# Two transformer parts on one core: attention tasks spaced by one step, a later request for a norm factor, another order in the channel sums

## The chip, the core and the metric

The kernel runs on one core of a Trainium2 chip. TensorE (PE) multiplies matrices, VectorE (DVE) and ScalarE (ACT) work element by element, GpSimd (POOL) does a few small powers, and SyncE (SP) starts the weight transfers. Each engine takes its instructions in program order and waits on semaphores where an operand or a buffer isn't ready. The metric is the time of one execution on the device, in microseconds; the kernel before has been timed in three runs.

## What is computed

The input is 256 tokens of width 1024 in float32. Two blocks follow each other. The first has two layers, each an attention and a gated feed-forward net with a convolution over three tokens; the second layer's attention has 16 query heads, 4 key heads, a window of 128 tokens and a learned "sink" in the softmax. The second block mixes a gated delta rule with a retention and ends with a plain feed-forward net; the change touches it only in one sum.

```python
def rmsnorm(x, g):
    xf = x.astype(jnp.float32)
    y = xf * lax.rsqrt(jnp.mean(xf * xf, axis=-1, keepdims=True) + EPS)
    return (y * g.astype(jnp.float32)).astype(x.dtype)
...
    m = jnp.maximum(jnp.max(logits, axis=-1, keepdims=True), sink)
    e = jnp.exp(logits - m)
    p = e / (jnp.sum(e, axis=-1, keepdims=True) + jnp.exp(sink - m))
    out = jnp.einsum('bkgnqp,bknpd->bkgnqd', p.astype(v.dtype), vcat)
...
    u = conv_b + sum(conv_w[j] * up[:, j:j + S_] for j in range(CONV_W))
    gate, val = jnp.split(u, 2, axis=-1)
    return (jax.nn.silu(gate) * val) @ w_down
...
        x = x + o.transpose(0, 2, 1, 3).reshape(B_, S_, N_HEADS * HEAD_DIM) @ w_o
        x = x + conv_ffn(rmsnorm(x, ffn_norm[l]), w_up[l], conv_w[l], conv_b[l], w_down[l])
```

## The kernel before

**Weights.** Every weight comes by DMA in halves of 512 KB (`raw`). ACT rounds a half to `hi` (L192), DVE takes the rest as `lo` (L201, two instructions of 512 columns a half), and PE multiplies three times: hi by high part, hi by low part, lo by high part of the other operand (`OH`/`OL` or `XH`/`XL`). A chunk of weights is four *pieces*; a piece is 12 matmuls of 128 x 256 (L138). The pieces form one long list, in the order in which PE takes them.

**Tasks beside the list.** All else (norms, attention, gates) is written as Python generators. After every piece each active generator is advanced by one step; `pause(n)` lets n pieces go by. So the numbers in the tables at the top of the file are delays in pieces, and the order on each queue comes from them.

**Attention.** `attend` handles a pair of heads. A task first waits `delay + 1` steps (`N_AD0` for the first attention, `N_AD1` for the second). Then, in one step: *qk*, the scores on PE, two banks; the masked maximum on DVE (L625, an instruction and a read of its result, four times, then `nm`, L629); the exponentials on ACT (L633), and for the second attention the sinks' (`es`, L637). Two steps later comes the scaling *S* on DVE (sum with `es` L641, reciprocal L643, four multiplications L146). A step later *T*: six transposes on PE (L149), which ACT copies to `pT` (L142). A step later *PV* on PE, a copy `o` and its rounding `OH` on ACT (L142, L467), and another step later `OL` on DVE (L469). `e` and `pT` lie in one ring of tiles, "h", of `HB` = 6. The second attention's eight tasks belong to four chunks of queries of two tasks each; a chunk's tasks begin when its product is finished and DVE has rotated it (*rope*, L582 to L585, into `qk`).

**Norms.** The squares of the channels are summed over partitions by matmuls with a column of ones: `sum_ch`, for each half of the tokens (`t`) and each quarter of it (`j`, 32 tokens), adds up the three parts that `Norm` keeps. `stat` computes the factor from the sum: DVE (`tok`, L536), POOL (`RTOK`, a power, L537); then it pauses `N_STAT[n]` steps, PE transposes RTOK to a row (L149), and ACT copies it to `RB` (L541). The four factors of the first block are n0, nf0 (ahead of the first net), n1 and nf1, with `N_STAT[1]` to `[4]`; the second block begins with a double one, `stat2`, and has nmix later.

**Deferred posts and banks.** While a factor is under way, finished products can't be scaled: `wpost` puts their follow-up into `deferred`, and the next post after the factor is there, `late`, does them all. `wbank` gives the next chunk a bank of the set `ps_w` as long as fewer than two posts are deferred, and of the set `ps_d` otherwise. In the first net the follow-up of a chunk (`act`) is the multiplication by `RB` (L763), the convolution (ACT L789, DVE L793), the gate (ACT L796, DVE L798) and the split.

Of the kernel before, what the change touches and what calls it, by code (L numbers as in the profile page):

```python
# [18 lines left out]
def pause(n):  # L19
    for _ in range(n):  # L20
        yield
# [4 lines left out]
EPS = 1e-6  # L26
LEVELS = 5
LA = 3
HB = 6
RAW = 4  # L30

N_RN = (0, 1, 1, 5)
N_SY = (0, 6, 4, 4, 3)
N_STAT = (0, 3, 5, 2, 5)
N_AD0 = (4, 0, 0, 0, 0, 0, 0, 2)
N_AD1 = (3, 2, 1, 3, 0, 0, 2, 0)
N_CONV4 = (0, 1, 2, 2)
N_M1 = (1, 1, 2, 3)
MAGIC = 12582912.0
# [27 lines left out]
def body(ctx: ExitStack, tc: tile.TileContext, a):  # L67
# [10 lines left out]
    def TW(shape, tag, bufs=2, dt=F32):  # L78
        return wk.tile(shape, dt, name=tag, tag=tag, bufs=bufs)

    side = {"n": 0, "dbusy": False}
# [3 lines left out]
    def PT(tag="side"):  # L85
        if tag == "side":

            age = {t: taken[t][-BANKS[t]] if len(taken[t]) >= BANKS[t] else 0 for t in "sd"}
            tag = "s" if side["dbusy"] or deferred or age["s"] <= age["d"] else "d"
        side["n"] += 1  # L90
        taken[tag].append(side["n"])
        return ps.tile([128, 512], F32, name="ps_" + tag, tag=tag, bufs=BANKS[tag])
# [12 lines left out]
    def P_(n, i=None):  # L105
        lo, hi = PRM_O[n]
        return prm[:, lo:hi] if i is None else prm[:, lo + i:lo + i + 1]

    def C_(n):
        lo, hi = CST_O[n]  # L110
        return cst[:, lo:hi]
# [25 lines left out]
    def mm(out, lhsT, rhs, start, stop):  # L137
        PE.matmul(out, lhsT, rhs, start=start, stop=stop, skip_group_check=True)  # L138

    def cp(eng, out, in_, scale=None):  # L140
        if eng == "S":
            S.activation(out, in_, AF.Copy, scale=scale) if scale is not None else S.copy(out, in_)  # L142
        elif scale is None:
            V.tensor_copy(out, in_)
        else:
            V.tensor_scalar(out, in_, scale, None, op0=OP.mult)  # L146

    def tr(out, in_):
        PE.transpose(out, in_, ident)  # L149
# [4 lines left out]
    parts = {}  # L154
    state = {"dma": 0, "hi": 0, "lo": 0, "part": 0}
    where, last_of = {}, []
    deferred = []
# [102 lines left out]
    def drain(gen):  # L260
        while gen in active:
            step(gen)
# [12 lines left out]
    def free(*tags):  # L275
        for t in tags:
            used[t] -= 1

    def wbank(more=0):

        if len(deferred) + more >= 6:
            drain(cur["stat"])
            late()
        return PT("w" if len(deferred) + more < 2 else "d")

    def waiting():
        return cur["stat"] in active or cur.get("kv") in active

    def late(n=99):
        while deferred and n:  # L290
            deferred.pop(0)()
            n -= 1
# [21 lines left out]
    def W_chunk(src, xs, post, pre=None, bank=None):  # L314
        def m(ck, s, hi, lo):
            xh, xl = xs
            if s == 0:
                ck.bank = PT(bank) if bank else wbank()
            todo = []
            for kk in range(2):  # L320
                k = 2 * s + kk
                for f in range(2):
                    c = slice(kk * 256 + f * 128, kk * 256 + f * 128 + 128)
                    todo.append((ck.bank[:, f * T:(f + 1) * T], hi[:, c], lo[:, c], xh[:, k], xl[:, k], k == 0 and f == 0, k == 7))
            products(todo, s == 0 and 0)
        return add(Chunk(src, 2048, 4, m, pre, {3: lambda ck: wpost(post)(ck.bank)}))

    def X_chunk(src, xs, post, pre=None):
        def m(ck, s, hi, lo):
            xh, xl = xs  # L330
            if s == 0:
                ck.bank = wbank()
            todo = []
            for kk in range(2):
                k = 2 * s + kk
                for t in range(2):
                    c = slice(kk * T, kk * T + T)
                    tt = slice(t * 128, t * 128 + 128)
                    todo.append((ck.bank[:, t * T:(t + 1) * T], xh[:, k, tt], xl[:, k, tt], hi[:, c], lo[:, c], k == 0 and t == 0, k == 7))
            products(todo, True)  # L340
        return add(Chunk(src, 2048, 4, m, pre, {3: lambda ck: wpost(post)(ck.bank)}))
# [115 lines left out]
    def slots(t):  # L457
        return OH[:, t % 16], OL[:, t % 16]
# [6 lines left out]
    def split(src, hi, lo):  # L465

        S.activation(hi, src, AF.Copy)  # L467
        yield
        V.tensor_tensor(lo, src, hi.bitcast(F32), op=OP.subtract)  # L469


    class Norm:
# [16 lines left out]
        def sums(self, out):  # L489
            sum_ch(out, [self.acc[:, :T], self.sq[:, :T], self.sq[:, T:]])  # L490

    def sum_ch(out, parts):

        for t in range(2):
            for j in range(0, 128, 32):
                for i, x in enumerate(parts):
                    c = t * 128 + j
                    mm(out[j:j + 32, t:t + 1], x[:, c:c + 32], ones, i == 0, i == len(parts) - 1)

# [29 lines left out]
    def stat(norm):  # L529
# [7 lines left out]
        G.tensor_tensor(RTOK, m, mhalf[:, :2], op=OP.pow)  # L537
        yield from pause(N_STAT[n])
        p = PT("s")
# [70 lines left out]
    def attend(q, k, v, slot, window=False, sink=None, delay=0, done=False):  # L610

        yield from pause(delay + 1)
        mx = TW([128, 4], "mx", 4)
        nm = TW([128, 4], "nm", 4)
        sums = TW([128, 4], "sums", 4)
        e = [TW([128, 384], "h", HB) for _ in range(2)]
        qbs = ((0, slice(0, 128), MW[:, 128:256]), (1, slice(128, 384), MW if window else MF))
        for h in range(2):
            r = slice(64 * h, 64 * h + 64)
            b = PT()  # L620
            mm(b[:, 0:128], q[r, 0:128], k[r, 0:128], True, False)
            mm(b[:, 128:384], q[r, 128:256], k[r, 0:256], True, False)
            for qb, c, m in qbs:
                i = 2 * h + qb
                V.tensor_tensor_reduce(e[h][:, c], b[:, c], m, 0.125, -3e38 if sink is None else P_("sinks", sink + h),  # L625
                                       op0=OP.add, op1=OP.max, accum_out=mx[:, i:i + 1])
        if done:
            free("qk")
        V.tensor_scalar(nm, mx, -1.0, None, op0=OP.mult)  # L629
        for h in range(2):  # L630
            for qb, c, _ in qbs:
                i = 2 * h + qb
                S.activation(e[h][:, c], e[h][:, c], AF.Exp, bias=nm[:, i:i + 1], accum_out=sums[:, i:i + 1])  # L633
        if sink is not None:
            es = TW([128, 4], "es", 4)
            for h in range(2):
                S.activation(es[:, 2 * h:2 * h + 2], nm[:, 2 * h:2 * h + 2], AF.Exp,  # L637
                             bias=P_("sinks", sink + h))
        yield from pause(2)
        if sink is not None:  # L640
            V.tensor_tensor(sums, sums, es, op=OP.add)  # L641
        ri = TW([128, 4], "ri", 4)
        V.reciprocal(ri, sums)  # L643
        for h in range(2):
            for qb, c in ((0, slice(0, 128)), (1, slice(128, 384))):
                i = 2 * h + qb
                cp("V", e[h][:, c], e[h][:, c], ri[:, i:i + 1])
        yield from pause(1)
        pT = [TW([128, 384], "h", HB) for _ in range(2)]
        for h in range(2):  # L650
            b = PT()
            for i in range(3):
                tr(b[:, i * 128:i * 128 + 128], e[h][:, i * 128:i * 128 + 128])

            cp("S", pT[h], b[:, :384])
        yield from pause(1)
        b = PT()
        for h in range(2):
            o = slice(64 * h, 64 * h + 64)
            mm(b[o, 0:256], v(0, h), pT[h][:, 0:256], True, False)  # L660
            mm(b[o, 128:256], v(1, h), pT[h][:, 256:384], False, True)
        o = TW([128, T], "e")
        cp("S", o, b[:, :T])
        yield from split(o, *slots(slot))
# [187 lines left out]
    def q1_task(c, bank):  # L852
# [4 lines left out]
        for i in range(2):  # L857
# [3 lines left out]
                                  (lambda kt: lambda t, h: VB[:, t, (2 * kt + h) * 64:(2 * kt + h) * 64 + 64])(kt),  # L861
                                  p, True, 2 * p, N_AD1[p], i == 1))

# [415 lines left out]
    def ret_task(h):  # L1279
# [7 lines left out]
        free("qn", "qn")  # L1287
        sT = TW([128, 384], "h", HB)
        dw = C_("decw")[:, h * T:h * T + T]
# [492 lines left out]
def build(nc, arrays):  # L1782
    a = {k: nc.dram_tensor("in_" + k, v.shape, mybir.dt.from_np(v.dtype), kind="ExternalInput").ap()
         for k, v in arrays.items()}
    a["out"] = nc.dram_tensor("out_x", (2, 128, D), F32, kind="ExternalOutput").ap()
    with tile.TileContext(nc) as tc:
        body(tc, a)
# [12 lines left out]
```

## Time and profile before

| | |
|---|---|
| three runs, us | 1318.57 (median), 1314.76, 1320.49 |
| profiled execution, us | 1320.17 |
| its span, us | 1317.7 |
| PE / weight loads / DVE / ACT busy | 98% / 94% / 74% / 55% |
| mean granted clock of PE | 0.995 |
| chain that ended last | PE 91%, DVE 5%, ACT 2%, issue 1% |

The span is the stretch from the first to the last instruction; the execution's own time is 2.5 us longer. The chain that ended last follows the work back from the end, at each step to what released it. By the timeline the first net's sum nf0 is at 132 us and the second attention's first scores at 340; the second net's long sum is at 597, and the second block follows.

### The profile page before, as it was taken

The numbers are of one execution on the slowest core, as the hardware profiler recorded it, in microseconds if no ns is written. First come the engines' busy times: TensorE is split into PE (matmuls) and PEld (weight loads), VectorE is DVE, ScalarE is ACT, GpSimd is POOL, SyncE is SP. The second block draws the span as 40 slices with busy tenths as digits, with TensorE's granted clock in tenths as the row PEclk, the third lists the DMA queues.
The fourth block names the chain that finished last, engine by engine and source line by source line (L and its number), as shares of the span: only waits on it lengthen the run. The fifth ranks groups of instructions, "written<-read, shape, count | busy, mean of one in ns | idle before, by whom it ended". The sixth has DMA issues, their size and how long they took to land.

```text
span 1317.7 us, 28944 instructions
## 1 busy us (share of the span) xinstructions
PE 1290.7 (98%) x11824; PEld 1233.9 (94%) x11824; DVE 973.8 (74%) x2149; ACT 725.5 (55%) x1158; POOL 28.0 (2%) x32
## 2 busy tenths in 40 slices
PE   7999999998999999999999999999999999999998
PEld 6989999998889999998989999999999999899996
DVE  6998887778888977787778889575648556855554
ACT  5666665555665755566554454354334445655553
POOL 0000000000000000000000000000000000000000
PEclk9999999999999999999999999999999999999999
DMA  7435565554324655544333333346454554465552
GB/s 243 144 130 169 189 209 185 188 192 161 107 102 154 214 185 184 192 153 155 129 129 114 113 130 129 129 160 207 139 183 166 183 195 156 159 215 191 193 184 88
DMA packets 60468, 215.77 MB, mean 164 GB/s; under 512 B 6832, under 2 KB 7600, under 8 KB 60336
## 3 DMA queue, kind: packets, MB, share of 16 engines
q1 hardware_dynamic: 59328, 212.31, 48.4%
q8 instruction: 92, 1.51, 0.5%
q10 hardware_dynamic: 1008, 1.63, 0.4%
q14 instruction: 40, 0.33, 0.1%
HBM read 212.86 MB, written 1.05 MB: 162 GB/s over the span
## 4 chain that ended last, share of the span: by engine, by line
PE 91%; DVE 5%; ACT 2%; issue 1%; DMA 0%; POOL 0%; SPq 0%; POOLq 0%; DVEq 0%; ACTq 0%
PE ps_w L138 53%; PE ps_d L138 32%; PE ps_s L138 4%; PE ps_s L149 1%; DVE lo L201 1%; PE ps_d L149 1%; ACT h L633 1%; DMA xT<-in_x 0%; ACT hi L192 0%; DVE y L793 0%; DVE OL L690 0%; DVE XL L463 0%; DVE h L625 0%; DVE y L1399 0%; DVE REG L146 0%
## 5 line engine op out<-in xcount | busy, mean ns | idle before, releaser
L201 DVE TENSOR_TENSOR lo<-raw,hi 128x512 fp32r<-128x512 f32 x801 | 520.4, 685 | 99.2 <-ACT hi L192 98.5
L192 ACT ACTIVATE hi<-raw 128x1024 fp32r<-128x1024 f32 (+1 forms) x403 | 418.8, 1048 | 167.6 <-PE ps_w L138 81.1
L138 PE MATMUL ps_w<-XH,hi 128*128 128x256 f32 x976 | 164.4, 290 | 4.4 <-ACT hi L192 1.9
L138 PE MATMUL ps_w<-XL,hi 128*128 128x256 f32 x976 | 154.5, 280 | 0.5 <-DVE XL L1475 0.5
L138 PE MATMUL ps_w<-XH,lo 128*128 128x256 f32 x976 | 154.0, 279 | 0.0
L138 PE MATMUL ps_w<-OH,hi 128*128 128x256 f32 x896 | 144.4, 283 | 0.0
L138 PE MATMUL ps_w<-OH,lo 128*128 128x256 f32 x896 | 141.9, 280 | 0.4 <-DVE lo L201 0.4
L138 PE MATMUL ps_w<-OL,hi 128*128 128x256 f32 x896 | 142.0, 280 | 0.0
L138 PEld LDWEIGHTS ps_w<-XH,hi 128*128 128x128 f32 x976 | 132.7, 189 | 8.7 <-ACT hi L192 3.4
L138 PEld LDWEIGHTS ps_w<-XL,hi 128*128 128x128 f32 x976 | 131.5, 189 | 0.9 <-DVE XL L1475 0.9
L138 PEld LDWEIGHTS ps_w<-XH,lo 128*128 128x128 f32 x976 | 131.3, 189 | 0.0
L138 PE MATMUL ps_d<-OH,hi 128*128 128x256 f32 x776 | 125.2, 282 | 0.0
L138 PEld LDWEIGHTS ps_w<-OH,hi 128*128 128x128 f32 x896 | 120.8, 189 | 3.6 <-issue 3.5
L138 PE MATMUL ps_d<-OL,hi 128*128 128x256 f32 x776 | 123.5, 279 | 0.0
L138 PE MATMUL ps_d<-OH,lo 128*128 128x256 f32 x776 | 123.3, 279 | 0.0
L138 PEld LDWEIGHTS ps_w<-OH,lo 128*128 128x128 f32 x896 | 120.9, 189 | 0.7 <-DVE lo L201 0.6
L138 PEld LDWEIGHTS ps_w<-OL,hi 128*128 128x128 f32 x896 | 120.9, 189 | 0.0
L138 PEld LDWEIGHTS ps_d<-OH,hi 128*128 128x128 f32 x776 | 104.1, 187 | 1.9 <-issue 1.7
L138 PEld LDWEIGHTS ps_d<-OL,hi 128*128 128x128 f32 x776 | 104.1, 187 | 0.4 <-DVE OL L469 0.2
L138 PEld LDWEIGHTS ps_d<-OH,lo 128*128 128x128 f32 x776 | 104.1, 187 | 0.2
L789 ACT ACTIVATE y<-u,prm 128x256 f32<-128x256 f32 x88 | 48.0, 596 | 60.1 <-DVE u L763 60.1
L763 DVE TENSOR_TENSOR u<-ps_w,RB 128x512 f32<-128x512 f32 x44 | 30.2, 692 | 60.1 <-PE ps_w L138 53.8
(372 smaller groups left out, 1608.4 us busy)
## 6 DMA issues: line engine op xcount, KB each, us to landing
raw<-in_wu SPq DMA_DIRECT2D x108, 512.0 KB, 4.2
raw<-in_wd SPq DMA_DIRECT2D x68, 512.0 KB, 4.0
raw<-in_wgb SPq DMA_DIRECT2D x24, 512.0 KB, 3.9
raw<-in_wqk SPq DMA_DIRECT2D x16, 512.0 KB, 3.9
raw<-in_wza SPq DMA_DIRECT2D x16, 512.0 KB, 4.0
raw<-in_wqkb SPq DMA_DIRECT2D x16, 512.0 KB, 4.2
raw<-in_wbra SPq DMA_DIRECT2D x16, 512.0 KB, 3.8
raw<-in_wbrb SPq DMA_DIRECT2D x16, 512.0 KB, 4.6
```

The source lines that it names most:

```text
L138: PE.matmul(out, lhsT, rhs, start=start, stop=stop, skip_group_check=True)
L149: PE.transpose(out, in_, ident)
L192: S.activation(hi[:, :w], raws[n][:, :w], AF.Copy)
L201: V.tensor_tensor(lo[:, c], raws[n][:, c], hi[:, c].bitcast(F32), op=OP.subtract)
L633: S.activation(e[h][:, c], e[h][:, c], AF.Exp, bias=nm[:, i:i + 1], accum_out=sums[:, i:i + 1])
L763: V.tensor_tensor(u, v2(bank), bc(RB, 2), op=OP.mult)
L789: S.activation(y[:, i], u[:, i], AF.Identity, bias=P_(cb, t), scale=P_(cw, 3 * t + 2))
```

## The change

The diff is whole. `HB`: the ring of `e` and `pT` grows by two tiles. `N_STAT[2]`: nf0's factor is transposed and copied three pieces later. `N_AD1` and the pause in `attend`: the eight tasks of the second attention get other delays, and S comes three steps behind qk where it came two behind. `wbank`, `hot`, `late`: after several deferred posts have been done, and no down-projection holds the `ps_d` banks, the next two requests for a bank may be met from `ps_d`. `sum_ch`: the loop over the parts is outside, the loop over the quarters inside. From L284 on, the line numbers of the changed kernel are up to 7 higher.

```diff
--- before.py
+++ after.py
@@ -26,14 +26,14 @@
 EPS = 1e-6
 LEVELS = 5
 LA = 3
-HB = 6
+HB = 8
 RAW = 4
 
 N_RN = (0, 1, 1, 5)
 N_SY = (0, 6, 4, 4, 3)
-N_STAT = (0, 3, 5, 2, 5)
+N_STAT = (0, 3, 8, 2, 5)
 N_AD0 = (4, 0, 0, 0, 0, 0, 0, 2)
-N_AD1 = (3, 2, 1, 3, 0, 0, 2, 0)
+N_AD1 = (1, 2, 3, 4, 0, 2, 0, 2)
 N_CONV4 = (0, 1, 2, 2)
 N_M1 = (1, 1, 2, 3)
 MAGIC = 12582912.0
@@ -281,12 +281,19 @@
         if len(deferred) + more >= 6:
             drain(cur["stat"])
             late()
+        if hot and not deferred:
+
+            hot.pop()
+            return PT("d")
         return PT("w" if len(deferred) + more < 2 else "d")
+
+    hot = []
 
     def waiting():
         return cur["stat"] in active or cur.get("kv") in active
 
     def late(n=99):
+        hot[:] = [0, 0] if len(deferred) > 1 and not side["dbusy"] else []
         while deferred and n:
             deferred.pop(0)()
             n -= 1
@@ -492,8 +499,8 @@
     def sum_ch(out, parts):
 
         for t in range(2):
-            for j in range(0, 128, 32):
-                for i, x in enumerate(parts):
+            for i, x in enumerate(parts):
+                for j in range(0, 128, 32):
                     c = t * 128 + j
                     mm(out[j:j + 32, t:t + 1], x[:, c:c + 32], ones, i == 0, i == len(parts) - 1)
 
@@ -636,7 +643,7 @@
             for h in range(2):
                 S.activation(es[:, 2 * h:2 * h + 2], nm[:, 2 * h:2 * h + 2], AF.Exp,
                              bias=P_("sinks", sink + h))
-        yield from pause(2)
+        yield from pause(2 if sink is None else 3)
         if sink is not None:
             V.tensor_tensor(sums, sums, es, op=OP.add)
         ri = TW([128, 4], "ri", 4)
```

Three places show what moves. First DVE at the start of the first net, from the norm sum's `tok` on. `u<-ps_w,RB` is the first multiplication by the factor, `y<-u,prm,y` the convolution, `e<-e,y` the gate. Before:

```order
L536 TENSOR_SCALAR tok_1777<-ps_s 128x2
L201 TENSOR_TENSOR lo<-raw,hi 128x512 x5
L763 TENSOR_TENSOR u<-ps_w,RB 128x512 x2
L201 TENSOR_TENSOR lo<-raw,hi 128x512 x2
L793 SCALAR_TENSOR_TENSOR y<-u,prm,y 128x255 x2
L793 SCALAR_TENSOR_TENSOR y<-u,prm,y 128x254 x2
L793 SCALAR_TENSOR_TENSOR y<-u,prm,y 128x255 x2
L793 SCALAR_TENSOR_TENSOR y<-u,prm,y 128x254 x2
L798 TENSOR_TENSOR e<-e,y 128x256 x2
L763 TENSOR_TENSOR u<-ps_d,RB 128x512
L201 TENSOR_TENSOR lo<-raw,hi 128x512
```

Changed:

```order
L543 TENSOR_SCALAR tok_1777<-ps_s 128x2
L201 TENSOR_TENSOR lo<-raw,hi 128x512 x8
L770 TENSOR_TENSOR u<-ps_w,RB 128x512 x2
L800 SCALAR_TENSOR_TENSOR y<-u,prm,y 128x255 x2
L800 SCALAR_TENSOR_TENSOR y<-u,prm,y 128x254 x2
L800 SCALAR_TENSOR_TENSOR y<-u,prm,y 128x255 x2
L800 SCALAR_TENSOR_TENSOR y<-u,prm,y 128x254 x2
L805 TENSOR_TENSOR e<-e,y 128x256 x2
L770 TENSOR_TENSOR u<-ps_d,RB 128x512
L201 TENSOR_TENSOR lo<-raw,hi 128x512
```

Eight `lo` stand ahead of the first use of RB where five stood, and the two behind it are gone.

Second, ACT in the second attention, from the fourth task's last exponential on (`h_4552` before, `h_4568` now). `COPY h_` is a task's `pT`, with ps_d or ps_s as the bank of its transposes. Before:

```order
L633 ACTIVATE h_4552,sums_4550<-h_4552,nm_4549 128x256
L637 ACTIVATE es_4568<-nm_4549,prm_74 128x2 x2
L142 COPY h_4594<-ps_d_4596 128x384
L142 COPY h_4595<-ps_d_4601 128x384
L192 ACTIVATE hi_4607<-raw_4407 128x1024
L142 COPY h_4628<-ps_s_4630 128x384
L142 COPY h_4629<-ps_s_4635 128x384
L142 COPY e_4645<-ps_d_4640 128x256
```

Changed:

```order
L640 ACTIVATE h_4568,sums_4566<-h_4568,nm_4565 128x256
L644 ACTIVATE es_4584<-nm_4565,prm_74 128x2 x2
L192 ACTIVATE hi_4588<-raw_4407 128x1024
L142 COPY h_4602<-ps_d_4604 128x384
L142 COPY h_4603<-ps_d_4609 128x384
L142 COPY e_4650<-ps_s_4645 128x256
L474 ACTIVATE OH_71<-e_4650 128x256
```

A `hi` now stands between the fourth exponential and the first task's copies.

Third, DVE in the second attention, ahead of the fifth task's scaling. The `mx` rows are the end of the sixth task's reductions, `STREAM_SHUFFLE` to `qk<-y,u` a rope. Before:

```order
L625 ISA h,mx<-ps_s,MW,prm 128x256
L625 ISA mx 128x1
L629 TENSOR_SCALAR nm<-mx 128x4
L201 TENSOR_TENSOR lo<-raw,hi 128x512
L469 TENSOR_TENSOR OL<-e,OH 128x256 x2
L201 TENSOR_TENSOR lo<-raw,hi 128x512
L641 TENSOR_TENSOR sums<-sums,es 128x4
L643 RECIPROCAL ri<-sums 128x4
L146 TENSOR_SCALAR h<-h,ri 128x128
L146 TENSOR_SCALAR h<-h,ri 128x256
```

Changed:

```order
L632 ISA h,mx<-ps_s,MW,prm 128x256
L632 ISA mx 128x1
L636 TENSOR_SCALAR nm<-mx 128x4
L589 STREAM_SHUFFLE u<-ps_w 128x512
L590 TENSOR_TENSOR y<-ps_w,CR 128x512
L591 TENSOR_TENSOR u<-u,SR 128x512
L592 TENSOR_TENSOR qk<-y,u 128x512
L201 TENSOR_TENSOR lo<-raw,hi 128x512
L476 TENSOR_TENSOR OL<-e,OH 128x256
L648 TENSOR_TENSOR sums<-sums,es 128x4
L650 RECIPROCAL ri<-sums 128x4
L146 TENSOR_SCALAR h<-h,ri 128x128
```

The rope of the next chunk now stands ahead of the fifth task's scaling, directly behind the sixth task's reductions.

## Rows read from the trace of the kernel before

**Rows 1.** Page, part 1: busy time, share of the span, instructions.

```profile
PE 1290.7 (98%) x11824; PEld 1233.9 (94%) x11824; DVE 973.8 (74%) x2149; ACT 725.5 (55%) x1158; POOL 28.0 (2%) x32
```

**Rows 2.** By stretches: window, length; busy PE, PEld, DVE, ACT, POOL; clock; DMA; GB/s.

```profile
145.00:310.00 165.00, 165.00 (x1417) 165.00 (x1416) 136.74 (x277) 100.25 (x149) 0.00 (x0) 1.00 0.56 187
...
340.00:390.00 50.00, 46.89 (x377) 39.17 (x377) 41.36 (x157) 37.61 (x121) 0.00 (x0) 1.00 0.30 104
```

**Rows 3.** PE: chain, first net; then timeline, second attention (start, us, work, [idle before]).

```profile
165.19 11.20 PE ps_w L138 x96
...
339.96 0.93 PE L138 MATMUL ps_d<-REG,qk 64*128 64x128 f32 x8
...
342.44 0.93 PE L138 MATMUL ps_d<-REG,qk 64*128 64x128 f32 x8
...
350.24 0.63 PE L138 MATMUL ps_w<-OH,lo 128*128 128x256 f32 x4
...
351.95 1.16 PE L149 MATMUL ps_s<-cst,h 128*128 128x128 f32 x6 [1.08 <-DVE h L146]
...
353.44 1.24 PE L138 MATMUL ps_d<-h,REG 128*64 128x256 f32 x8 [0.33 <-ACT h L142]
```

**Rows 4.** Sums of channels on PE: pieces of the chain, then the timeline.

```profile
406.05 0.91 PE ps_s L138 x48
...
597.36 1.63 PE ps_s L138 x96
...
656.26 0.43 PE L138 MATMUL ps_d<-ones,sqq 128*32 128x1 f32 x32
```

**Rows 5.** PE timeline, behind the sum n1.

```profile
324.21 0.69 PE L149 MATMUL ps_s<-cst,RTOK 128*128 128x128 f32 x2 [2.42 <-POOL RTOK L537]
```

**Rows 6.** First feed-forward net: DVE timeline, and one PE row (last).

```profile
140.42 1.29 DVE L763 TENSOR_TENSOR u<-ps_w,RB 128x512 f32<-128x512 f32 x2 [3.32 <-ACT RB L541]
...
150.71 1.29 DVE L201 TENSOR_TENSOR lo<-raw,hi 128x512 fp32r<-128x512 f32 x2
...
152.25 0.69 DVE L763 TENSOR_TENSOR u<-ps_w,RB 128x512 f32<-128x512 f32 x1
...
157.50 0.69 DVE L763 TENSOR_TENSOR u<-ps_w,RB 128x512 f32<-128x512 f32 x1
...
151.96 0.63 PE L138 MATMUL ps_w<-OH,lo 128*128 128x256 f32 x4
```

**Rows 7.** DVE timeline, second attention.

```profile
340.92 0.35 DVE L625 CUSTOM_DVE_ANT_0 h<-ps_d,MW,prm 128x128 f32<-128x128 f32 x1 [1.29 <-PE ps_d L138]
...
342.47 0.87 DVE L146 TENSOR_SCALAR REG<-ps_w,RTOK 128x256 f32<-128x256 f32 x2
...
349.04 0.35 DVE L625 CUSTOM_DVE_ANT_0 h<-ps_d,MW,prm 128x128 f32<-128x128 f32 x1
...
355.80 0.74 DVE L582 STREAM_SHUFFLE u<-ps_w 128x512 f32<-128x512 f32 x1
...
358.35 0.69 DVE L201 TENSOR_TENSOR lo<-raw,hi 128x512 fp32r<-128x512 f32 x1
```

**Rows 8.** ACT timeline, second attention.

```profile
345.54 0.40 ACT L633 ACTIVATE h<-h,nm 128x128 f32<-128x128 f32 x1 [0.70 <-DVE nm L629]
...
347.69 1.04 ACT L192 ACTIVATE hi<-raw 128x1024 fp32r<-128x1024 f32 x1
...
352.93 0.83 ACT L142 COPY h<-ps_d 128x384 f32<-128x384 f32 x2
```

**Rows 9.** Granted clock (PEclk) of PE by stretches, and the PE row at 620.92.

```profile
324.00:327.00 3.00, 2.79 (x13) 0.50 0.64 175
...
351.90:354.00 2.10, 1.72 (x10) 1.00 0.00 0
...
621.00:624.00 3.00, 3.00 (x14) 0.50 0.40 157
...
620.92 1.17 PE L138 MATMUL ps_w<-XH,hi 128*128 128x256 f32 x4 [1.91 <-ACT hi L192]
```

## The prediction, made before the changed kernel was run

> **What bounds the kernel now.** The page's busy line is read first: TensorE (PE) is busy 98% of the span [rows 1]. So an edit counts only if it changes how many microseconds PE works, how long it waits, or its clock. The table by stretches comes next [rows 2]: in the first feed-forward net (145 to 310 us) PE is busy for all 165.0 us and VectorE (DVE) for 136.7; in the second attention (340 to 390) PE is idle for 3.1 of 50 us. The edits stand at just these places, and in the norms' sums. The timelines of single engines there are read last. A weight piece is 12 matmuls; 96 take 11.20 us [rows 3], so a piece is 1.40 and a third of it .47. I count a wait from start to start: the third begun at 350.24 is over for PE at 350.71, and the transposes begin at 351.95, 1.24 later (bracketed: 1.08) [rows 3]. Counted so, the six waits of the second attention are 3.9 us, where the window shows 3.1 idle.
>
> **Sums by quarters.** In a sum of three parts neighbouring matmuls go to the same quarter of the output; its 24 matmuls, 48 records, take .91 us of chain, of which .10 is the end of the last: 17 ns a record. The 48 matmuls of the second net's end take 1.63 [rows 4]. In the new order the quarter changes with every matmul. One sum has that order already, since it has one part: its 32 records lie .43 from the first's start to the last's end; less the .17 that one takes, .26 for 31 steps, 8.4 ns [rows 4]. So 24 matmuls go from .81 to .40, saving .41; this holds for n0, nf0, nf1 and nmix, and the 96 records save .72: 4 x .41 + .72 = 2.4 us. The sum n1 saves nothing: PE waits 2.42 us after it for the row RTOK from GpSimd [rows 5], whose input comes from DVE, where it is queued behind `lo`s and not behind the sum. If that were wrong it would be 2.8; if interleaved groups cost what neighbours cost, 0. I take 2.4, since the row of the same instruction in the new order exists.
>
> The Trainium skill, page "TensorE: Matmul & The Clock Gate", section "Part 3: Packing small matmuls — row/col tiling", says of packed small matmuls that a weight load overlaps matmuls in flight only where the row group differs; here every matmul uses all rows and only the columns change, so by that rule the term would be 0 and the sum 2.4 us higher. The row of the one-part sum, 8.4 ns against 17 [rows 4], speaks against it.
>
> **The norm factor asked for later (nf0).** Before, PE transposes RTOK after two pieces on the d banks; ScalarE (ACT) copies RB, and DVE, idle for 3.32 us, starts the deferred gates at 140.42 [rows 6] and is then without a gap. Now three more pieces go ahead: RB comes 3 x 1.40 = 4.2 us later. PE did not wait there, so nothing is removed. DVE has three `lo` of .60 to do meanwhile, 1.8 us; it therefore falls 2.4 us back. What covers that is how far `lo` runs ahead of its use: at its narrowest the first of the pair begun at 150.71 (.60 each, the second's end at 152.00) ends at 151.4 and PE uses it at 151.96, .56 us later [rows 6]. DVE needs 5.25 us a chunk (152.25 to 157.50 [rows 6]) where PE needs four pieces, 5.60, so it does not make the loss good before that place. 2.4 - .56 = 1.84, **+1.9 us** with the hand-over, as a new PE wait around 150 to 160, behind DVE's conv steps. Bounds: 2.5 with no cover, and 0 if the leads are longer than this place's; I take 1.9, by the row of this very place.
>
> **The banks.** The new `hot` rule is set by `late` with several deferred posts and cleared by the next `late` with none, before a bank is asked for; in the built order only the fourth chunk's pair goes to the d banks, by the old rule of two deferred. No instruction is added, and pieces on either bank follow each other alike. Nothing.
>
> **The longer ring.** HB 8 allows a fourth task's reduction ahead of the third's transposes. Before, it starts at 349.04, and its row has no idle time of DVE ahead of it [rows 7]: DVE came to it from its own scaling. So the ring cost nothing, and more of it gives nothing.
>
> The Trainium skill, "Perfetto Trace Analysis", section "Identifying Performance Opportunities", says that a gap that keeps repeating on the engine to be saturated can mean too few buffers. By that the waits were the ring's and would go (first rival); the row of 349.04 speaks against it.
>
> **Tasks a step apart.** PE's instructions are the same: eight times qk, T (transposes) and PV, and 16 weight pieces in between. Only waits change. Durations: qk and the piece behind it 2.48 (339.96 to 342.44) [rows 3]; T about .6. On DVE: the first reduction .96 after qk's start (340.92), reductions and nm 1.55 (to 342.47), `lo` .60, rope 2.55 (355.80 to 358.35); T follows .75 after the scaling S begins (half of S's 1.48, four multiplications of .25 and two small steps) [rows 7]; OL .34. On ACT: exp 2.15 (345.54 to 347.69), hi .94; PV starts .51 after the first copy (352.93 to 353.44) [rows 3, 8]. I laid the three queues end to end in the new order with these; the same laying of the old order gives before's waits within .2.
> - First PV. Before, its copies start 12.97 us after the first qk (339.96 to 352.93), held by the fourth exp. Now a `lo` (.60) stands ahead of the fourth reduction, and ACT has a hi (.94) between that exp and the copies: PV at 12.97 + .60 + .94 + .51 = 15.0. PE is ready after four qk with their pieces, a T and a piece: 4 x 2.48 + .6 + 1.5 = 12.0. Wait 3.0 by this sum, 2.3 by the laying: taken 2.7, in place of 1.24 and some .3 before the first T's and PV's.
> - Fifth T. Its scaling now stands behind the sixth task's reductions, the rope of the next chunk, a `lo` and an OL. From the sixth qk: .96 + 1.55 + 2.55 + .60 + .34 + .75 = 6.75; PE is ready after qk and two pieces, 2.48 + 1.40 = 3.88. Wait 2.9, laid 2.8, in place of .5.
> - Eighth qk. Its bank is free when the sixth task's copies are done, which stand on ACT behind the seventh exp, O and OH (.7) and a hi: .96 + 1.55 + 2.15 + .7 + .94 + .73 = 7.0 from the seventh qk; PE comes there after some 5.6 (two pieces of 1.6, qk, PV, T). Wait 1.2 to 1.5, taken 1.3, new.
> - Seventh qk .2, fourth PV .3, last PV .3 by the laying. The old waits at the sixth and seventh T go.
>
> Together 7.6 against 3.9: **+3.7 us**, from -3.4 (first rival) to 5.
>
> **The clock.** PE's granted clock is 0.50, the level of 1.2 GHz, behind the idles of 2.42 us at 324.21 and of 1.91 at 620.92 [rows 5, 9]; behind the 1.08 at 351.95 it is 1.00 [rows 3, 9]. Each such stretch lasts 3.4 us and does half the work; PE's idle parts in it taken off, it costs some 1.7 us where PE is the bound. The first PV's wait (2.3 to 3.0) and the fifth T's (2.8) are in the size that dips. Behind the fifth T a slower PE meets the eighth qk's wait, which shrinks by what PE is late, so of the two I count **one: +1.7** (0 to 3.4).
>
> **The sum.** 3.7 + 1.7 + 1.9 - 2.4 = +4.9 us. The profiled execution took 1320.17, so 1325.1; the median of the three runs is 1318.57, 1.6 lower, so **1323.5**.
>
> **Rivals.**
> 1. *The waits go*: the second attention's waits all but go (-3.4), the later factor is covered by a `lo` lead that I read too short (0), sums -2.4: 1312.8. For it: PE has a piece after nearly every step, so each task gets more time. Against: DVE had no gap in the old bunch from 342.47 to 358.35 [rows 7], and the new order puts rope and reductions of later tasks ahead of scalings. Chance .12.
> 2. *The order costs half*: attention +1.9 without a dip, nf0 +.6, sums -2.4: +.1, 1318.7. For it: a wait early in a bunch gives DVE and ACT a lead that the later ones use; my terms partly count one lag twice. Chance .20.
> 3. *Slower by the clock*: both long idles, at the first PV and the fifth T, drop the clock and neither stretch is absorbed, and nf0 has no cover: 3.7 + 3.4 + 2.5 - 2.4 = +7.2, 1325.8. It decides where the bracketed idles reach 1.91, the shorter of the two that dipped [rows 9]. For it: both of mine are above that. Against: the eighth qk's wait. Chance .20.
> 4. The forecast, .48; its own range 1320 to 1327.
>
> **How the numbers follow.** 0.5%, about what a measurement of this kernel can tell, is 6.6 us: 1312.0 and 1325.2. Faster: half of rival 1, .05. Slower: most of rival 3 and a quarter of the forecast, .31. The rest, .64, within. One in ten is left out below 1314 (most of rival 1) and one above 1328.5 (rival 3 with a term more).
>
> **What would show it.** Right: the chain pieces of the sums at .5 and, for the long one, .9; PE idles of 2 to 3 us before the first PV and the fifth T of the second attention, released by ACT's `h` copy and DVE's `h` scaling; 0.50 for 3 us behind at least one; one wait of 1 to 2 us for DVE's `lo` early in the first net. Wrong: PE idle in the second attention not over the 3.1 us of before [rows 2]; sums at .9 as before; no wait in the first net. If that idle time is under 1, the laying of the queues fell, and rival 1 is the case.

## The result, and the profile after

The changed kernel takes 1326.93 us (median of 5 runs, 1326.87 to 1332.51), the kernel before 1316.22 (5 runs, 1313.67 to 1320.49). The ratio is 1.009, 95% interval 1.0073 to 1.0106: it is slower, by 10.7 us between the medians. Its profiled execution took 1326.87 us with a span of 1325.0, 6.7 and 7.3 us more than the one of before.

The page's busy line and two rows of the table by stretches (window, length, busy time of PE, weight loads, DVE, ACT and POOL, then clock, DMA share and GB/s), to set beside [rows 1, 2]:

```profile
PE 1292.6 (98%) x11824; PEld 1233.9 (93%) x11824; DVE 974.2 (74%) x2149; ACT 725.2 (55%) x1158; POOL 27.8 (2%) x32
...
145.00:310.00 165.00, 163.15 (x1392) 162.35 (x1391) 136.57 (x277) 100.38 (x149) 0.00 (x0) 1.00 0.55 186
340.00:395.00 55.00, 47.87 (x359) 39.58 (x358) 40.88 (x155) 35.65 (x115) 0.00 (x0) 0.94 0.26 86
```

The page says nearly the same as before: 98% busy, the same instructions. The stretches say more. The first net has 1.85 us without PE where it had none, and the second attention has 7.1 us idle of 55 where it had 3.1 of 50, at a mean clock of 0.94.

The sums, as pieces of the chain (start, length, work; some records are missing, so the counts are below 48 and 96), to set beside [rows 4], and the wait behind n1, to set beside [rows 5]:

```profile
415.70 0.51 PE ps_s L138 x47
605.01 0.91 PE ps_s L138 x77
```

```profile
324.71 0.43 PE L149 MATMUL ps_s<-cst,RTOK 128*128 128x128 f32 x2 [2.43 <-POOL RTOK L544]
```

.91 has become .51, and 1.63 has become .91. At n1 the saving was given back: from the start of that sum to the row above are 6.49 us in both traces (317.72 to 324.21 before, 318.22 to 324.71 now). It did not go into the wait behind, 2.43 for 2.42, but into the two pieces between: from the first third of the one to the last of the other are 2.92 us where they were 2.52, and one weight load there waits .21 for DVE's `OL`.

The first net: all bracketed waits of PE between 145 and 310 us, then the chain at the second of them (which engine the path ran on), to set beside [rows 6]:

```profile
148.84 0.73 PE L138 MATMUL ps_w<-OH,lo 128*128 128x256 f32 x4 [0.54 <-DVE lo L201]
150.37 0.74 PE L138 MATMUL ps_w<-OH,hi 128*128 128x256 f32 x4 [0.80 <-ACT hi L192]
153.28 0.73 PE L138 MATMUL ps_w<-OH,lo 128*128 128x256 f32 x4 [0.30 <-DVE lo L201]
157.95 0.74 PE L138 MATMUL ps_w<-OH,lo 128*128 128x256 f32 x4 [0.21 <-DVE lo L201]
```

```profile
147.58 0.61 DVE u L770
...
148.28 1.09 ACT y L796 x2
149.37 0.96 ACT hi L192
```

Counted from start to start the four are .70, .96, .46 and .37, together 2.5 us. Three are for `lo`, as forecast, and make 1.5. The longest is for a `hi` that stands on ACT behind the convolution's first step of the next chunk, and that step behind DVE's `u`.

The second attention: the first qk, the marked waits and the work behind the fifth T, on PE, to set beside [rows 3]:

```profile
341.63 0.93 PE L138 MATMUL ps_d<-REG,qk 64*128 64x128 f32 x8
...
351.77 1.16 PE L149 MATMUL ps_d<-cst,h 128*128 128x128 f32 x6 [0.22 <-DVE h L146]
...
357.62 1.24 PE L138 MATMUL ps_s<-h,REG 128*64 128x256 f32 x8 [3.29 <-ACT h L142]
...
368.72 1.25 PE L138 MATMUL ps_d<-h,REG 128*64 128x256 f32 x8 [0.56 <-ACT h L142]
...
376.65 1.59 PE L149 MATMUL ps_s<-cst,h 128*128 128x128 f32 x6 [2.82 <-DVE h L146]
378.17 2.29 PE L138 MATMUL ps_s<-REG,qk 64*128 64x128 f32 x8
380.39 1.22 PE L138 MATMUL ps_d<-OH,hi 128*128 128x256 f32 x4
...
386.61 1.30 PE L138 MATMUL ps_s<-REG,qk 64*128 64x128 f32 x8 [0.24 <-ACT h L142]
```

The two long waits stand where the prediction put them, before the first PV (3.36 from start to start, with the .55 that a piece's last third takes ahead of a PV) and before the fifth T (2.98). Behind the first, PE goes on at once at its full speed; behind the second, the qk takes 2.29 us, not .9. The granted clock (PEclk, the column behind PE's busy time) of these stretches, and of the one behind n1:

```profile
325.20:331.90 6.70, 5.64 (x27) 0.50 0.42 135
357.60:361.00 3.40, 3.38 (x26) 1.00 0.00 1
376.65:383.10 6.45, 6.45 (x26) 0.50 0.22 81
```

Between the starts of the sums the two profiled executions differ like this: from n0's sum on, -.4 to nf0's, +2.5 to n1's, +1.2 to the first qk, +8.0 to nf1's, -2.0 to the long sum, -.4 and +.1 for the rest; and -1.5 before n0's sum. The -1.5 and the +1.2 are half-clock stretches that one execution had and the other not, or longer (before: 3.4 us at 17 us and 3.4 behind n1; after: none and 6.8). The rest hides another one, of 3.4 us from 1137.5 on, that only the changed kernel's execution had. Most of the -2.0 is another cadence in the second net, 11.31 us for 96 matmuls before and 11.20 after.

### The profile page after: what moved, and what is told of

The parts are those of the page before. It is cut to its first block, busy times and chain, and to the rows that moved or that the text cites. A ratio compares the mean times of both kernels' runs of the same rounds, so it can differ in the third digit from the quotient of the medians.

```text
span 1325.0 us, 28929 instructions
## 1 busy us (share of the span) xinstructions
PE 1292.6 (98%) x11824; PEld 1233.9 (93%) x11824; DVE 974.2 (74%) x2149; ACT 725.2 (55%) x1158; POOL 27.8 (2%) x32
## 3 DMA queue, kind: packets, MB, share of 16 engines
q10 hardware_dynamic: 1008, 1.63, 0.4%
## 4 chain that ended last, share of the span: by engine, by line
PE 89%; DVE 6%; ACT 2%; issue 1%; DMA 0%; POOL 0%; SPq 0%; POOLq 0%; DVEq 0%; ACTq 0%
PE ps_w L138 51%; PE ps_d L138 32%; PE ps_s L138 4%; DVE lo L201 1%; PE ps_s L149 1%; DVE y L800 1%; PE ps_d L149 1%; ACT hi L192 0%; DMA xT<-in_x 0%; ACT h L640 0%; DVE h L632 0%; ACT y L796 0%; DVE u L770 0%; DVE OL L697 0%; DVE XL L470 0%
## 5 line engine op out<-in xcount | busy, mean ns | idle before, releaser
L138 PE MATMUL ps_w<-OH,hi 128*128 128x256 f32 x880 | 141.3, 283 | 0.8 <-ACT hi L192 0.8
L138 PE MATMUL ps_w<-OL,hi 128*128 128x256 f32 x880 | 138.9, 280 | 0.0
L138 PE MATMUL ps_d<-OH,hi 128*128 128x256 f32 (+1 forms) x792 | 128.0, 282 | 0.0
L138 PE MATMUL ps_d<-OH,lo 128*128 128x256 f32 (+1 forms) x792 | 126.0, 280 | 0.0
L138 PE MATMUL ps_d<-OL,hi 128*128 128x256 f32 (+1 forms) x792 | 126.0, 280 | 0.0
L138 PEld LDWEIGHTS ps_d<-OH,hi 128*128 128x128 f32 (+1 forms) x792 | 106.6, 188 | 2.9 <-issue 2.7
L138 PEld LDWEIGHTS ps_d<-OL,hi 128*128 128x128 f32 (+1 forms) x792 | 106.7, 188 | 0.2
L138 PEld LDWEIGHTS ps_d<-OH,lo 128*128 128x128 f32 (+1 forms) x792 | 106.7, 188 | 0.2
L800 DVE SCALAR_TENSOR_TENSOR y<-u,prm,y 128x254 f32<-128x254 f32 (+1 forms) x176 | 73.1, 480 | 0.1
```

What stands on the lines that cost most here:

```text
L800: V.scalar_tensor_tensor(y[:, i, s:], u[:, i, :T - s], P_(cw, 3 * (j + 22 * i) + 2 - s), y[:, i, s:], op0=OP.mult, op1=OP.add)
```

## Experiments

Each run was timed beside the kernel before on the same chip, and the ratio compares the two sets of executions. It is not the ratio of the two medians shown: for x1 the medians differ by 2.8 us, the ratio stands for 1.6.

| run | median us | before us | ratio | 95% interval |
|---|---|---|---|---|
| the changed kernel | 1326.93 | 1316.22 | 1.0090 | 1.0073 to 1.0106 |
| x1: second attention as before | 1319.83 | 1317.02 | 1.0012 | 0.9999 to 1.0025 |
| x2: only the second attention changed | 1326.48 | 1317.02 | 1.0072 | 1.0053 to 1.0091 |
| x3: only the sums changed | 1315.72 | 1317.02 | 0.9985 | 0.9971 to 0.9998 |
| x4: changed, nf0's factor early | 1325.14 | 1317.02 | 1.0063 | 1.0049 to 1.0076 |
| y1: changed, pause 2 | 1321.22 | 1317.77 | 1.0031 | 1.0018 to 1.0043 |
| y2: changed, second half's delays old | 1325.17 | 1317.77 | 1.0057 | 1.0041 to 1.0073 |
| y3: changed, first half's delays old | 1324.55 | 1317.77 | 1.0050 | 1.0034 to 1.0067 |
| x8: before, ring of 8 | 1316.60 | 1317.77 | 0.9991 | 0.9976 to 1.0006 |
| z1: other delays, sums, nf1 later | 1314.94 | 1316.88 | 0.9987 | 0.9975 to 0.9998 |
| z2: z1 and n1 later | 1314.10 | 1316.88 | 0.9984 | 0.9973 to 0.9995 |

### Which part makes the loss: x1 and x2

x1 takes the second attention back and keeps the rest:

```diff
-HB = 8
+HB = 6
-N_AD1 = (1, 2, 3, 4, 0, 2, 0, 2)
+N_AD1 = (3, 2, 1, 3, 0, 0, 2, 0)
-        yield from pause(2 if sink is None else 3)
+        yield from pause(2)
```

Expected: 

> The changed kernel with the second attention as before (delays 3,2,1,3,0,0,2,0, pause 2, ring of 6); the later norm factor, the bank rule and the new sum order stay. Theory: the second attention makes the loss (its stretch from the first qk to the sum nf1 grew by 8.0 us between the two traces), so this is 2.5 us (waits for lo and hi in the first net) less 2.8 us (sums) from before: 1316 us, within 0.2% of before, and the second attention's waits are 3.9 us again. Rival, the loss is in the first net and in the clock dips that move with it: 1322 or more.

x2 makes the same edit the other way in the kernel before.

Expected: 

> The kernel before with only the second attention changed (delays 1,2,3,4,0,2,0,2, pause 3, ring of 8). Theory: +8 us against before, 1324 us: waits of about 3.4 before the first PV and 3.0 before the fifth T (7.6 in all against 3.9), and a stretch at the half clock behind at least one of the two. Rival, the loss needs the first net's later factor: within 3 us of before.

x1 stays near before (1.0012, an interval from -.1 to 3.3 us), x2 is slower by 9.5 us (1.0072). So the second attention makes the loss, and it needs nothing else of the change. x1's median, 1319.83, missed the expected 1316; the later factor's 2.5 less the sums' 2.0 (x3, below) makes .5, which lies in the interval, and the rival's 1322, 5 us above before, does not. In x1 its waits are those of before again: PE's bracketed waits there are 1.08, .33, .35, .52 and .71, for 1.08, .33, .34, .52 and .72. In x2 the two long waits are there as in the changed kernel, and here both of them are followed by half the clock:

```profile
356.11 1.92 PE L138 MATMUL ps_s<-h,REG 128*64 128x256 f32 x8 [3.28 <-ACT h L142]
```

```profile
355.40:358.00 2.60, 1.89 (x9) 0.50 0.11 46
358.00:362.00 4.00, 4.00 (x20) 0.50 0.32 89
379.30:382.50 3.20, 3.20 (x15) 0.50 0.48 164
```

The same PV that took 1.24 us in the changed kernel's trace takes 1.92.

### The sums alone: x3

```diff
-            for j in range(0, 128, 32):
-                for i, x in enumerate(parts):
+            for i, x in enumerate(parts):
+                for j in range(0, 128, 32):
```

Expected: 

> The kernel before with only the sums' order changed. Theory: 24 matmuls in .41 instead of .81 us, 48 in .81 instead of 1.53, so 2.4 us less on the path, 1313.8 us, and the five bursts show it; at n1 the wait for RTOK grows by .4 and gives it back. Rival, the sums' saving is taken back by later waits or by the clock: within 1 us of before.

In the chain of x3 the sums are as short as in the changed kernel:

```profile
406.40 0.51 PE ps_s L138 x46
...
595.79 0.91 PE ps_s L138 x75
```

By the ratio the time is .9985 of before, 2.0 us less, with an interval from .3 to 3.8 (1.3 us by the medians); the expected 2.4 lies within, the rival's 0 to 1 isn't excluded by the time, though the pieces show where it comes from. The expected longer wait at n1 did not come: it is 2.43 here too, and what was saved goes into the pieces ahead of it, as in the changed kernel.

### The later factor: x4

```diff
-N_STAT = (0, 3, 8, 2, 5)
+N_STAT = (0, 3, 5, 2, 5)
```

Expected: 

> The changed kernel with nf0's factor asked for after five pieces again. Theory: the four waits of the first net (148.84 to 157.95, 2.5 us together) go, 1324.4 us, and PE has no wait there. Rival, the waits come from the changed bank of the fourth chunk or are absorbed later: within 1 us of the changed kernel's 1326.9.

In x4's trace PE has no bracketed wait between 130 and 170 us, and x1, which keeps the later factor beside the old attention, has the four again (.53, .80, .30, .20). So the four waits come from the later factor alone. The median of x4 is 1.8 us below the changed kernel's, but the two were not timed together, and the intervals of their ratios overlap, so the size rests on the traces.

### What makes the two long waits: y1, y2 and y3

y1 undoes the third step between qk and the scaling:

```diff
-        yield from pause(2 if sink is None else 3)
+        yield from pause(2)
```

Expected: 

> The changed kernel with the scaling two steps behind the scores again (pause 2); delays 1,2,3,4,0,2,0,2, ring of 8 and all else stay. Theory: the third step puts the rope and the sixth task's reductions ahead of the fifth task's scaling; with two steps the wait of 3.0 us before the fifth T shrinks below .6 and the half clock behind it goes, the wait before the first PV stays at 2 to 3.4: 1323 us (the changed kernel's 1326.9 less 2.5 of waits and some 1.7 of clock). Rival, the spacing alone makes both waits: 1326 to 1328 and 3.0 us before the fifth T.

y2 and y3 take back one half of the delays each:

```diff
-N_AD1 = (1, 2, 3, 4, 0, 2, 0, 2)
+N_AD1 = (1, 2, 3, 4, 0, 0, 2, 0)
```

Expected: 

> The changed kernel with the delays of the last four tasks as before (1,2,3,4,0,0,2,0), pause 3. Theory: the two long waits have separate causes, so the one before the first PV stays at 3.4 us and the one before the fifth T falls below 1: 1323 us. Rival, the second half's waits are late consequences of the first: the wait before the fifth T stays near 3.

```diff
-N_AD1 = (1, 2, 3, 4, 0, 2, 0, 2)
+N_AD1 = (3, 2, 1, 3, 0, 2, 0, 2)
```

Expected: 

> The changed kernel with the delays of the first four tasks as before (3,2,1,3,0,2,0,2), pause 3. Theory: the wait before the first PV comes from the lo and the hi that the first half's spacing puts ahead of it and falls to 1.5 us or less; that before the fifth T stays at 2.5 to 3: 1325 us. Rival as for the run with the first half alone: both go or both stay.

The waits of over .5 us on PE, in y1 (all tasks spaced, two steps):

```profile
353.35 1.24 PE L138 MATMUL ps_s<-h,REG 128*64 128x256 f32 x8 [1.12 <-ACT h L142]
358.49 1.24 PE L138 MATMUL ps_d<-h,REG 128*64 128x256 f32 x8 [1.70 <-ACT h L142]
371.59 1.22 PE L149 MATMUL ps_s<-cst,h 128*128 128x128 f32 x6 [0.69 <-DVE mx L632]
375.10 1.24 PE L138 MATMUL ps_s<-h,REG 128*64 128x256 f32 x8 [0.89 <-ACT h L142]
```

in y2 (first four spaced):

```profile
358.14 1.92 PE L138 MATMUL ps_s<-h,REG 128*64 128x256 f32 x8 [3.28 <-ACT h L142]
373.86 1.93 PE L138 MATMUL ps_s<-h,REG 128*64 128x256 f32 x8 [1.92 <-ACT h L142]
```

and in y3 (last four spaced):

```profile
352.20 1.16 PE L149 MATMUL ps_d<-cst,h 128*128 128x128 f32 x6 [0.88 <-DVE h L146]
356.08 1.24 PE L138 MATMUL ps_d<-h,REG 128*64 128x256 f32 x8 [0.66 <-ACT h L142]
373.43 1.59 PE L149 MATMUL ps_s<-cst,h 128*128 128x128 f32 x6 [2.60 <-DVE h L146]
```

The causes are separate: the first half's spacing makes the wait before the first PV (3.28 in y2, .66 in y3), the second half's makes that before the fifth T (2.60 in y3, in y2 that T has no bracket). y2 has a new wait of 1.92 at the fourth PV in its place. At their full length both need the third step: in y1 the scaling stands ahead of the sixth task's reductions and the rope on DVE again, and the fifth T waits .69, by its bracket for one of those reductions (`mx`) and not for the scaling. The first PV waits 1.12 there, where 2 to 3.4 was expected: that half of the expectation was wrong. And the spacing itself isn't free with two steps: the second PV waits 1.70, and y1 is still slower than before (1.0031) with no half-clock stretch in its second attention. From the first qk to the last PV it takes 51.97 us, before 48.81. The third step beside all the old delays was not run, and no run moved a single `hi`, `lo` or rope: which instruction makes a wait is read from the order of the queues.

### The ring and the bank rule

x8 is the kernel before with `HB = 8`.

Expected: 

> The kernel before with the ring of e and pT grown from 6 to 8 and nothing else; every engine's instructions stay in their order. Theory: no task waited for the ring, so the second attention's six waits stay within .1 us of before's (1.24, .32, .50, .69, .88, .29) and the time is that of before within .2%. Rival, the waits were the ring's: up to 3.9 us less, 1313 us.

```profile
350.22 1.16 PE L149 MATMUL ps_s<-cst,h 128*128 128x128 f32 x6 [0.92 <-DVE h L146]
351.82 1.24 PE L138 MATMUL ps_d<-h,REG 128*64 128x256 f32 x8 [0.44 <-ACT h L142]
366.45 1.16 PE L149 MATMUL ps_s<-cst,h 128*128 128x128 f32 x6 [0.34 <-DVE h L146]
368.13 0.92 PE L149 MATMUL ps_s<-cst,h 128*128 128x128 f32 x6 [0.52 <-ACT h L142]
379.57 1.16 PE L149 MATMUL ps_s<-cst,h 128*128 128x128 f32 x6 [0.71 <-DVE h L146]
```

The first wait is .16 shorter than in [rows 3], the second .11 longer, both a little beyond the expected .1; the others are the same: the waits were not the ring's. The new spacing can't be run with the old ring, since with six tiles its tasks wait for one another in a circle. The change without the bank rule needs no run: without `hot` every engine's instructions are the same in the same order, with the same banks.

### Towards a faster version: z1 and z2

z1 puts other delays beside the new order of the sums, and nf1's sum a piece later; z2 adds a third step at n1:

```diff
-N_SY = (0, 6, 4, 4, 3)
+N_SY = (0, 6, 4, 4, 4)
-N_AD1 = (3, 2, 1, 3, 0, 0, 2, 0)
+N_AD1 = (3, 1, 0, 3, 0, 0, 1, 2)
```

Expected: 

> The kernel before with the new order of the sums, the delays 3,1,0,3,0,0,1,2 in the second attention (pause 2, ring of 6 as before) and the sum nf1 asked for one piece later. Theory: the sums give 2.0 us, the delays shorten the second attention's waits from 3.9 to about 2.5 without a rope ahead of a scaling and without an idle of 2 us, the later sum nf1 takes away the .55 wait for lo in the second net: 1313 us. Rival, the waits move and the time is that of the sums alone, 1315.7 us.

```diff
-N_STAT = (0, 3, 5, 2, 5)
+N_STAT = (0, 3, 5, 3, 5)
```

Expected: 

> As the run with the delays 3,1,0,3,0,0,1,2, and the factor n1 transposed three pieces after its sum, not two. Theory: PE's idle time before the row of RTOK falls from 2.4 us to about 1, so the half clock that follows it in nearly all traces is gone, and 1.7 us or more with it: 1311.5 us. Rival, the idle time only moves behind the next product (DVE's rope waits for RB either way), the clock dips there, and nothing is gained.

z1's waits in the second attention are .87, .27, .35, .48 and .82 in brackets, 2.8 for 3.0: hardly shorter. The wait for `lo` in the second net, .38 at 428.51 in before, is gone, as expected. Its time (.9987) is that of the sums alone; the rival was right. z2 moved the idle time instead of removing it:

```profile
321.94 0.43 PE L149 MATMUL ps_s<-cst,RTOK 128*128 128x128 f32 x2 [1.03 <-POOL RTOK L537]
324.94 0.89 PE L138 MATMUL ps_w<-XH,hi 128*128 128x256 f32 x4 [2.57 <-DVE y L583]
```

```profile
325.50:328.50 3.00, 3.00 (x16) 0.50 0.38 154
```

1.03 before the row of RTOK, where it was 2.42, but 2.57 behind it, where it was 1.06 in before, and half the clock follows. The rival was right here too. z2 is the fastest version tried, by its ratio 2.1 us below before (.9984, interval .9973 to .9995); that it is faster than the sums alone isn't shown.

## Why the prediction was right, and where not

The forecast was 1323.5, 4.9 us over the median of the three runs known then; the measured time, 1326.9, lies in the range of 1314 to 1328.5 and at the edge of the forecast's own, 1320 to 1327. Against the medians of five runs it is 10.7 us more, and not 4.9. That was the second likeliest side: slower by over .5% had .31, within .5% had .64. The reasons were right in kind; the sum was too small by more than half. That the time still came within 3.4 us of the forecast is luck: the reference, 1318.57, was 2.4 above the later median, and from 1316.22 the same sum gives 1321.1, 5.8 too low.

**Sums: right.** Forecast .91 to .50 and 1.63 to .91, measured .51 and .91. n1's part was absorbed, as said, though not in the wait for RTOK. The section of the Trainium skill that was set against it ("TensorE: Matmul & The Clock Gate", "Part 3: Packing small matmuls — row/col tiling") would have had the bursts unchanged. All rows are used by every matmul here and the columns alternate, and a record takes half the time; the measurement decides. In the old order neighbours also add into the same output; no run separates that from the shared columns.

**The later factor: right in kind, 2.5 for 1.9.** The step counted DVE's lag and the lead of `lo`. It left out that ACT lags behind DVE in the same burst: the longest of the four waits is for a `hi`, behind the convolution's first step on ACT. The total meets the bound "no cover", 2.5, by another sum: 1.5 for `lo` and .96 for the `hi`. The sign "one wait of 1 to 2 us for DVE's `lo`" did not come; there are four waits, none over 1.

**Ring and banks: right**, nothing each (x8; the same instructions without the rule). The Trainium skill's remark in "Perfetto Trace Analysis", "Identifying Performance Opportunities", on gaps from too few buffers did not hold for these gaps: x8 has two tiles more in the ring and nearly the same gaps.

**The second attention's waits: nearly right in sum, 7.9 us for 7.6, not in each.** That is 4.0 more than before's 3.9, where +3.7 was forecast. The first PV waited 3.36, not 2.7. The hand-made sum took the `lo` ahead of the first scaling at its own .60; the trace shows that it also waited for its `hi`, which stands on ACT behind the second exponential (timeline of DVE, changed kernel):

```profile
350.42 0.69 DVE L201 TENSOR_TENSOR lo<-raw,hi 128x512 fp32r<-128x512 f32 x1 [1.11 <-ACT hi L192]
```

The fifth T waited 2.98 for 2.8, the fourth PV .64 for .3, and the eighth qk .25 for 1.3: PE came to it late, as the clock's paragraph said it might. The first T's (.38) and the last PV's (.31) make up the rest.

**A term left out.** The prediction said that PE's instructions are the same, and only waits change. They are, but a weight piece between two qk takes 1.61 (340.83 to 342.44 in before) and one between pieces 1.40. The old order changed 13 times from small work to weights, the new one 15 times. That makes some .4 us of the 7.8 by which the stretch from the first qk to the last PV grew (48.81 to 56.64 us: 4.0 waits, 3.3 clock, .5 left). This share is an estimate, not tested by a run.

**The clock: the step that failed in size.** One stretch of half clock was counted at 1.7 us. In the changed kernel's trace there was one, but 6.8 us long, and it cost 3.3: from the fifth T at 376.65 to the next PV at 383.22 are 6.57 us for a T, a qk and a piece, which take 3.3 at full speed (.81 for a T ahead of a qk, 361.81 to 362.62, and 2.48). In x2 and x4 both long waits were followed by half the clock:

```profile
353.20:359.60 6.40, 5.57 (x26) 0.50 0.22 68
377.00:383.50 6.50, 6.50 (x29) 0.50 0.26 81
```

These are x4's stretches; there the way from the first qk to the last PV took 59.6 us, 3.0 more than in the changed kernel's trace with the same waits. So by these traces the second attention loses 3.3 to 6.3 us to the clock, not 1.7, and the third rival (both waits drop the clock) was nearer than the forecast: its 3.4 us for the clock was still the cost of short stretches. With what the traces show (4.0 + .5 waits and changes, 3.3 to 6.3 clock, 2.5 first net, -2.4 sums) the sum is 7.9 to 10.9 us; the medians differ by 10.7.

**The reference point.** 1318.57 was the median of three runs; of five it was 1316.22. The profiled execution of before, 1320.17, was a long one: it had a half-clock stretch at its start and the slower cadence in the second net.

## What to carry to other kernels

Spacing tasks evenly on the bound engine is no gain by itself: what counts is which instructions of other tasks stand ahead of each hand-over on the engines that feed it, here, by the order of the queues, a `hi` ahead of the copies on ACT and a rope ahead of the scaling on DVE. When such a wait grows from 1 to 3 us, as here, its price on TensorE can be more than the wait alone: half the clock may follow it. An order of the three queues laid end to end with durations from the trace finds the places; the loads that feed a waiting instruction (`lo` behind its `hi`) must be in it.

## What the runs showed of the hardware that was not expected

The same idle time may or may not be followed by half the clock. Before the first PV PE idled 3.28 to 3.29 us in four traces (the changed kernel, x2, x4, y2); in three the granted clock was 0.50 behind it, in the changed kernel's 1.00 (the windows above, and in y2 the PV's 1.92 us). Behind n1 the idle was 2.42 to 2.44; 0.50 followed in ten of the eleven traces that have it, but in x1 the clock stayed at 1.00:

```profile
326.46 0.43 PE L149 MATMUL ps_s<-cst,RTOK 128*128 128x128 f32 x2 [2.44 <-POOL RTOK L544]
```

```profile
326.00:329.00 3.00, 1.83 (x14) 1.00 0.70 184
```

The wait of 1.9 us at 620.92 [rows 9] stands in all twelve traces, 1.85 to 2.05 us long. Half the clock followed in four (before, the changed kernel, x4, z1); in the other eight it stayed at 1.00, as in x1:

```profile
619.59 0.71 PE L138 MATMUL ps_w<-XH,hi 128*128 128x256 f32 x4 [1.92 <-ACT hi L192]
```

```profile
619.60:623.00 3.40, 3.40 (x29) 1.00 0.37 142
```

The stretches at 0.50 inside the work were 3.4 or 6.8 us long, in the same place of different executions either. So the third rival's condition, that the bracketed idles reach 1.91, read from [rows 5, 9], rested on too few rows. What decides it in a single execution stays open. It goes with much of the scatter of a kernel's runs: among the 23 executions of before that were timed beside y1, the two shortest (1313.2 and 1313.7 us) have a mean granted clock of .999, the two longest (1321.5 and 1322.1) one of .991.

A second thing stays open: 96 matmuls of a net take 11.20 or 11.31 us, constant through a net, and which of the two it is differs between traces of kernels that don't differ there (second net: 11.31 in before and x8, 11.20 in x1 and x3; first net: 11.31 in y1 and y3, 11.20 in y2).
